# Where transposed and split operands begin inside their SBUF tiles

## The chip, the core and the metric

The kernel runs on one core of a Trainium2 chip. Its time is the device time of one execution in microseconds (us). The engines that matter are TensorE (matmuls, and loads of the stationary operand, which the profile lists apart as PE and PEld), VectorE (DVE), ScalarE (ACT), GpSimd (POOL) and the DMA queues. Operands lie in SBUF, a memory of 128 partitions; a place in it is a byte address that holds for all partitions alike.

## What is computed

One layer of an encoder on a sequence of 512 positions with 1024 features, in float32: a feed-forward, a mixer, a second feed-forward, each between two norms, with residuals.

```
def swiglu(x, w_in, w_out):
    gate, up = jnp.split(x @ w_in, 2, axis=-1)       # 1024 -> 2 x 2816
    return (jax.nn.silu(gate) * up) @ w_out          # 2816 -> 1024

h = swiglu(rmsnorm(x, norm_ffn1_pre), w_ffn1_in, w_ffn1_out)
x = x + 0.5 * rmsnorm(h, norm_ffn1_post)
h = mixer(rmsnorm(x, norm_mix_pre), w_mix_in, ...)   # gated convolution and 4 mLSTM heads
x = x + rmsnorm(h, norm_mix_post)
h = swiglu(rmsnorm(x, norm_ffn2_pre), w_ffn2_in, w_ffn2_out)
x = x + 0.5 * rmsnorm(h, norm_ffn2_post)
```

The mixer multiplies its input by w_mix_in (1024 x 3088), makes y of a gated convolution (512 features) and of the heads (512 features), and multiplies y (512 x 1024) by w_mix_out.

## The kernel before

**Arithmetic.** Every large product is made of float32r matmuls: an operand is split in a high part (a cast on ScalarE, line 366) and a low part (a subtraction on VectorE, line 369), and high x high, high x low and low x high are summed in PSUM. Most products are in addition cut by Strassen's scheme, seven half-size products in place of eight.

**The matmuls, by line.** A matmul has a moving operand, whose columns stream through, and a stationary operand of 128 x 128, which is loaded first.

- L545 (`plain`) and L519 (`mm_part`) in the feed-forward: the moving operand is 256 columns of the transposed x, the stationary one a weight tile. x is kept in tiles of four rows (`q`) for each half of the features and of the sequence; a row holds 256 columns of the high part and then 256 of the low part. The loop over k goes through the four rows in turn. `xq_tile` hands these tiles out.
- L519 in `seven` and L510 (`mm_cols`) in the mixer: the same for the mixer's transposed x, with 256 and 512 columns. High and low parts have a tile each, marked by "m" in the dictionary.
- L953 (the mixer's v and gates): here the mixer's x is stationary, and the moving operand is a weight tile of rows of 528 columns, taken as 256 and 272 columns.
- L726 (`product_out`), the feed-forward's second product: the stationary operand is a "left factor", a split sum of blocks of the hidden layer, made by `left_a` and `left_b` into tiles from `halves`; the moving operand is 512 columns of the output weights. Two sets of left factors (i = 2 in `left_a` and i = 0 in `left_b`) lie in the pool of the residual instead (named xl in the profile).
- L748 (`mm_out`): the rest of that product without Strassen's scheme, its hidden blocks split into tiles `hs`.
- L1428: the mixer's output, with y stationary (`yc` of the convolution, `ym` of the heads) and 512 columns of w_mix_out moving.

**Order.** Matmuls of the feed-forward stand in the program's order where they are pinned; elsewhere a scheduler orders each engine's instructions when the program is built. DMAs of weights are issued from SP's queue, some of them from GpSimd's, ahead of use into a pool of four tiles (`raw`), and the splits go to a pool of twelve (`whi`, `wlo`, `ws`).

**Where tiles lie.** All these tiles have fixed buffers. The pool `big` has 13 buffers of four rows of 528 float32 (BW = 528), since the mixer's v weights need rows of 528. `bigt` takes the first 2048 columns of such a buffer as four rows of 512; `wide` gives the whole of it. The feed-forward's x takes `wide` as four rows of 528. The built program places the pools as follows, the same in both versions:

| pool | first byte of the first buffer | bytes from one buffer to the next | first byte modulo 256, all buffers |
|---|---|---|---|
| big (x, left factors, rest, y, v weights) | 24256 | 8448 | 192 |
| weights (whi, wlo, ws, wt) | 134080 | 4096 | 192 |
| residual and xl | 7872 | 4096 | 192 |

Stationary tiles of a weight buffer lie 512 bytes apart, so all of them start at 192 modulo 256.

The functions that the diff touches, and their callers:

Of the kernel before, what the change touches and what calls it, by code (L numbers as in the profile page):

```python
# [8 lines left out]
F32 = mybir.dt.float32  # L9
F32R = mybir.dt.float32r  # L10
# [26 lines left out]
BW = 528  # L37
# [4 lines left out]
def encoder_kernel(ctx: ExitStack, tc: tile.TileContext, a: dict, out: bass.AP):  # L42
# [16 lines left out]
    def nm(s):  # L59
        uid[0] += 1  # L60
        return f"{s}_{uid[0]}"

    def wide(dt=F32):
        return big.tile([P, 4 * BW], dt, tag="big", name=nm("big"))

    def bigt(dt=F32):
        return wide(dt)[:, 0:2048].rearrange("p (q f) -> p q f", q=4)

    def ps():
        return psum.tile([P, 512], F32, tag="ps", name=nm("ps"))  # L70
# [229 lines left out]
    def w_get(ahead=2):  # L300
        w_split(max(0, 1 + ahead - len(ready)))
        return ready.pop(0)


    def xtile():
        return xpool.tile([P, D], F32, tag="x", name=nm("x"))
# [58 lines left out]
    def split(hi, lo, src, eng=nc.vector):  # L365
        latest["hi"] = nc.scalar.copy(out=hi, in_=src)  # L366
        if pinned["act"]:
            pin(latest["hi"])
        latest["lo"] = eng.tensor_tensor(out=lo, in0=src, in1=f32(hi), op=ALU.subtract)  # L369
        pin(latest["lo"])  # L370
# [33 lines left out]

    def xq_tile(xq, key):
        if key not in xq["q"]:
            xq["q"][key] = bigt(F32R) if "m" in xq else wide(F32R).rearrange("p (q f) -> p q f", q=4)
        return xq["q"][key]

    def xq_hl(xq, key):  # L410
# [112 lines left out]
    def ffn(xq, between, finish, mid=None, within=None, ahead=(2, 2, 1, 1), late=None, prep=None, block=0):  # L523
# [56 lines left out]
        def hcol(k):  # L580
            return h[k // 4][:, k % 4, 0:512]
# [3 lines left out]

        def halves(g):
            if g == 1:
                t = bigt(F32R).rearrange("p q f -> p (q f)")
                return t[:, 0:1024].rearrange("p (g f) -> p g f", g=1), t[:, 1024:2048].rearrange("p (g f) -> p g f", g=1)
            return tuple(  # L590
                bigt(F32R).rearrange("p q f -> p (q f)")[:, 0:2048].rearrange("p (g f) -> p g f", g=2) for _ in range(2))

        def each(v, g):
            return [v[:, i] for i in range(g)]
# [9 lines left out]
        def left_a(i, home=None):  # L604
            g, a_, b_ = group(i)
            if home is None:
                hi, lo = halves(g)

                def put(c, v):
                    split_free(hi[:, :, c:c + v.shape[2]], lo[:, :, c:c + v.shape[2]], v)  # L610

                hi_, lo_ = each(hi, g), each(lo, g)
            else:
                hi_, lo_ = home

                def put(c, v):
                    for e in range(g):
                        split_free(hi_[e][:, c:c + v.shape[2]], lo_[e][:, c:c + v.shape[2]], v[:, e])

            def step1():  # L620
                s1 = t4()[:, 0:256 * g].rearrange("p (g f) -> p g f", g=g)
                tt(s1, a_[:, :, early], b_[:, :, early], ALU.subtract)
                put(256, s1)

            def step2():
                put(0, a_[:, :, later])
                tt(a_[:, :, early], a_[:, :, later], a_[:, :, early], ALU.subtract)

            def step3():
                tt(a_[:, :, later], a_[:, :, early], b_[:, :, early], ALU.add)  # L630
                put(768, a_[:, :, later])

            def step4():
                put(512, a_[:, :, early])

            out_ = parts(hi_, lo_, g, {1: 0, 5: 256, 7: 512, 6: 768})
            if home is not None:
                return [step1, step2, step3, step4], out_
            s1 = t4()[:, 0:256 * g].rearrange("p (g f) -> p g f", g=g)
            tt(s1, a_[:, :, early], b_[:, :, early], ALU.subtract)  # L640
            put(0, a_[:, :, later])
            tt(a_[:, :, early], a_[:, :, later], a_[:, :, early], ALU.subtract)
            tt(a_[:, :, later], a_[:, :, early], b_[:, :, early], ALU.add)
            put(256, s1)
            put(512, a_)
            return out_
# [72 lines left out]
        def product_out(n, left, right, first, last_):  # L719
            tb, half = bank[n]  # L720
            for t in range(2):
                if n == 4:
                    first = (t, 0) not in begun
                    begun.add((t, 0))
                for x, y in ((0, 0), (0, 1), (1, 0)):
                    nc.tensor.matmul(  # L726
                        acc[tb + t][half], left[n][x][:, blk(t)], right[n][y], start=first and x == y == 0,
                        stop=last_ and x == 1, skip_group_check=True)

        def taken(n):  # L730

            for t in range(2):
                o = acc[bank[n][0] + t][bank[n][1]]
                e12, e22, e21 = extra[2 + t, 1], extra[t, 1], extra[t, 0]
                if n == 1:
                    nc.scalar.copy(e12, o)
                elif n == 5:
                    tt(e22, o, e21, ALU.subtract, lambda v: (pin(v), mark.update(taken=v)))
                elif n == 6:
                    tt(e12, o, e12, ALU.subtract, pin)  # L740
                else:
                    tt(e21, o, e12, ALU.subtract, pin)

        def mm_out(tb, half, k, hT, w):
            fresh = (tb, half) not in begun
            begun.add((tb, half))
            for hh, ww in ((0, 0), (0, 1), (1, 0)):
                nc.tensor.matmul(  # L748
                    acc[tb][half], hT[hh][:, blk(tb)], w[ww][:, blk(half, 512)],
                    start=fresh and hh == ww == 0, stop=k == NF - 1 and hh == 1, skip_group_check=True)  # L750
# [13 lines left out]
        hs, plain_n = None, 0  # L764
        marks = []
        ks = {}
        for at, (kind, n) in enumerate(order):
            if kind == "k":
                if plain_n % 2 == 0:
                    hs = bigt(F32R)  # L770
                q = 2 * (plain_n % 2)
                plain_n += 1
                hT = (hs[:, q, 0:512], hs[:, q + 1, 0:512])
                split(hT[0], hT[1], hcol(n))
                ks[n] = (hT, w_get(min(2, len(order) - 1 - at)))
                if plain_n == 1 and mid:
                    mid()
                if n < NF - tail:
                    for tb, half in ((2, 0), (3, 0), (0, 1), (1, 1), (0, 0), (1, 0), (2, 1), (3, 1)):
                        mm_out(tb, half, n, *ks[n])  # L780
            elif kind == "a":
                marks.append(latest["lo"].ins)
                if n % 2 == 0 and n:
                    if n in soon:
                        lefts = soon[n]
                    else:
                        with tc.issue_after(marks[n - LAG]):
                            lefts = left_a(n)
                left, right = lefts[n % 2], w_get(1)
                for m in ((1, 6, 7, 5) if n else (6, 7, 5)):  # L790
                    product_out(m, left, right, n == 0, n == seven - 1)
                    if n == seven - 1:
                        taken(m)
                if n == TURN:
                    homes = [xpool.tile([P, D], F32R, tag="x", name=nm("xl")) for _ in range(4)]
                    with tc.issue_after(marks[n]):
                        soon["b"] = left_b(0, (homes[0:2], homes[2:4]))
            else:
                if n == 0:
                    lefts = soon["b"]  # L800
                elif n % 2 == 0:
                    with tc.issue_after(mark["taken"].ins):
                        lefts = left_b(n)
                left, right = lefts[n % 2], w_get(2)
                for m in (2, 3, 4):
                    product_out(m, left, right, False, False)
                if n == 1:
                    for tb in range(NT):
                        x_t[tb] = xtile()
                        nc.gpsimd.dma_start(x_t[tb], x_src[block][tb])  # L810
# [110 lines left out]
    def within1(tb):  # L921
        if tb >= 2:
            flip_m(tb - 2, st[tb - 2], st["xq"])

    ffn(
        xT1,
        {
# [4 lines left out]
    xq = st["xq"]  # L932
# [2 lines left out]
        return xq_hl(xq, (k // 4, tb // 2))[hl][:, k % 4, blk(tb % 2)]  # L935


    vaug = wide().rearrange("p (q f) -> p q f", q=4)
    vv = vaug.rearrange("p c (h e) -> p c h e", e=BW // 4)
    nc.gpsimd.memset(vv[:, :, :, DV:DV + 1], 1.0)  # L940
    spread = t2()
# [308 lines left out]
        pn2[:, 256:272], parl, acd.rearrange("p q c -> p (q c)"),  # L1250
        start=True, stop=True,
    )
    Ct = wide().rearrange("p (q f) -> p q f", q=4)
    Cf = Ct.rearrange("p q f -> p (q f)")
    Cs = Cf[:, 0:12 * 129].rearrange("p (q i e) -> p q i e", q=4, i=3)
    nat1 = Cf[:, 1552:2064].rearrange("p (c r) -> p c r", r=P)
# [8 lines left out]
    weigh_k()  # L1265
    weigh_q()
    plain_o(3)
    ym = (bigt(F32R), bigt(F32R))
    yc = (bigt(F32R), bigt(F32R))

    hs = {}

# [199 lines left out]
```

## Time and profile before

| | |
|---|---|
| median of 3 runs | 885.02 us (884.16 to 885.32) |
| profiled execution | 884.01 us, span of its instructions 882.1 us |
| mean granted TensorE clock | 0.998 |
| instructions | 15403, of them 6039 matmuls and 6039 loads of a stationary operand |
| DMA | 123.24 MB, mean 140 GB/s |

The span goes through the first feed-forward (to about 341 us, its second product from 232 us), the mixer (to about 546 us) and the second feed-forward (second product from 765 us). In rows of groups the number behind x counts instructions, and then come the busy time in us and the mean duration of one in ns. Matmuls overlap in the pipeline, so the mean duration of one is longer than the step from one to the next. In the chain in order of time a row is: start in us, length in us, engine, tile and line, count.

### The profile page before, as it was taken

To read this page: it belongs to the slowest core of one execution; us is meant where nothing else is said; L and a number is where in the kernel's file an instruction comes from. 1 tells how busy PE (TensorE), PEld (TensorE's weight loads), DVE (VectorE), ACT (ScalarE), POOL (GpSimd) and SP (SyncE) were. 2 spreads that over 40 slices of the span, in tenths; PEclk is the share of its full clock that TensorE was granted. 3 is DMA by queue.
4 is the path that set the end of the run, shared out by engine and by line. 5 is a ranking of instruction groups with operands and counts; after the bars stand their busy time and mean duration, and the time that the engine had idled before them with its cause. 6 is when DMAs were issued, how large, how long until landed. Compare 5 with 4: busy or idle time off the path is not lost.

```text
span 882.1 us, 15403 instructions
## 1 busy us (share of the span) xinstructions
PE 873.4 (99%) x6039; PEld 808.1 (92%) x6039; DVE 731.5 (83%) x1159; ACT 492.9 (56%) x855; POOL 93.6 (11%) x123
## 2 busy tenths in 40 slices
PE   8999999999999999999999999999999999999997
PEld 7999999999988889988998988999999999988885
DVE  7989898988889978887588757897898888869956
ACT  7655556544657645755475536555555555546722
POOL 5000000001232023100121011000000000223000
PEclk9999999999999999999999999999999999999999
DMA  9444333435998852442063733433333423899722
GB/s 263 121 121 134 106 95 98 120 88 130 227 246 200 279 180 86 121 119 72 1 191 96 223 112 106 130 100 97 96 96 98 138 77 109 202 243 229 268 74 95
DMA packets 140384, 123.24 MB, mean 140 GB/s; under 512 B 5500, under 2 KB 116112, under 8 KB 140312
## 3 DMA queue, kind: packets, MB, share of 16 engines
q1 hardware_dynamic: 129936, 97.62, 37.0%
q0 software_dynamic: 10368, 24.65, 12.6%
q8 instruction: 47, 0.77, 0.4%
q14 instruction: 25, 0.20, 0.1%
q10 hardware_dynamic: 8, 0.01, 0.0%
HBM read 115.96 MB, written 6.29 MB: 139 GB/s over the span
## 4 chain that ended last, share of the span: by engine, by line
PE 98%; DVE 0%; ACT 0%; issue 0%; POOL 0%; DVEq 0%; POOLq 0%; ACTq 0%
PE ps L519 48%; PE ps L726 19%; PE ps L510 9%; PE ps L545 5%; PE ps L1428 5%; PE ps L748 5%; PE ps L953 3%; PE ps L1331 1%; PE ps L422 1%; PE ps L1339 0%; PE ps L475 0%; PE ps L1280 0%; PE ps L1307 0%; PE ps L1300 0%; PE ps L1373 0%
## 5 line engine op out<-in xcount | busy, mean ns | idle before, releaser
L519 PE MATMUL ps<-big,whi 128*128 128x256 f32 x2064 | 284.1, 281 | 0.0
L519 PEld LDWEIGHTS ps<-big,whi 128*128 128x128 f32 x2064 | 261.4, 188 | 1.1 <-ACT t L1312 0.2
L366 ACT CAST whi<-raw 128x1024 fp32r<-128x1024 f32 x170 | 175.6, 1051 | 68.5 <-DVE raw L219 23.7
L369 DVE TENSOR_TENSOR wlo<-raw,whi 128x1024 fp32r<-128x1024 f32 x166 | 201.1, 1218 | 12.1 <-ACT whi L366 7.8
L519 PE MATMUL ps<-big,wlo 128*128 128x256 f32 x1032 | 161.8, 280 | 0.0
L519 PEld LDWEIGHTS ps<-big,wlo 128*128 128x128 f32 x1032 | 139.0, 189 | 0.0
L726 PE MATMUL ps<-whi,big 128*128 128x512 f32 x336 | 105.7, 389 | 0.0
L726 PEld LDWEIGHTS ps<-whi,big 128*128 128x128 f32 x336 | 62.9, 188 | 13.0
L519 PE MATMUL ps<-big,ws 128*128 128x256 f32 x516 | 70.0, 280 | 0.0
L173 POOL DMA_DIRECT2D raw<-in_w_ffn_out_dram x18 | 22.2, 1232 | 442.3 <-DMA raw<-in_w_ffn_out_dram 226.3
L519 PEld LDWEIGHTS ps<-big,ws 128*128 128x128 f32 x516 | 64.8, 188 | 0.0
L726 PE MATMUL ps<-wlo,big 128*128 128x512 f32 x168 | 64.8, 389 | 0.0
L693 ACT COPY t<-ps 128x256 f32<-128x256 f32 x40 | 14.9, 373 | 88.4 <-PE ps L519 88.4
L510 PE MATMUL ps<-big,whi 128*128 128x512 f32 x224 | 54.5, 394 | 0.0
L366 ACT CAST whi<-t 128x1024 fp32r<-128x1024 f32 (+1 forms) x44 | 39.5, 914 | 17.7 <-DVE t L219 10.2
L510 PEld LDWEIGHTS ps<-big,whi 128*128 128x128 f32 x224 | 41.4, 188 | 8.7
L369 DVE TENSOR_TENSOR wlo<-t,whi 128x1024 fp32r<-128x1024 f32 (+1 forms) x44 | 46.1, 1048 | 1.4 <-ACT whi L366 0.7
L748 PE MATMUL ps<-whi,big 128*128 128x512 f32 x128 | 39.8, 390 | 0.0
L726 PEld LDWEIGHTS ps<-wlo,big 128*128 128x128 f32 x168 | 31.5, 188 | 6.5
L695 DVE TENSOR_TENSOR t<-ps,t 128x256 f32<-128x256 f32 x40 | 16.9, 422 | 21.0 <-PE ps L519 20.9
L545 PE MATMUL ps<-big,whi 128*128 128x256 f32 x256 | 33.6, 282 | 0.0
L698 ACT ACTIVATE t<-t 128x512 f32<-128x512 f32 x40 | 25.2, 631 | 12.4 <-DVE t L695 12.0
(245 smaller groups left out, 1412.3 us busy)
## 6 DMA issues: line engine op xcount, KB each, us to landing
raw<-in_w_ffn_in_dram SPq DMA_DIRECT2D x68, 512.0 KB, 4.8
raw<-in_w_ffn_out_dram SPq DMA_DIRECT2D x26, 512.0 KB, 4.2
raw<-in_w_mix_in_dram SPq DMA_DIRECT2D x24, 512.0 KB, 4.2
t<-in_w_ffn_in_dram SPq DMA_DIRECT2D x20, 512.0 KB, 3.8
raw<-in_w_ffn_out_dram SPq DMA_DIRECT2D x36, 256.0 KB, 5.0
raw<-in_w_ffn_out_dram POOLq DMA_DIRECT2D x18, 512.0 KB, 7.8
xd<-x POOLq DMA_DIRECT2D x8, 512.0 KB, 2.9
x<-xd POOLq DMA_DIRECT2D x8, 512.0 KB, 5.2
```

The lines of the kernel that those rows point to most:

```text
L173: nc.gpsimd.dma_start(sums.rearrange("p (g f) -> p g f", g=2), top[:, 512:1024].rearrange("p (g f) -> p g f", g=1).broadcast_to([P, 2, 512 ...
L366: latest["hi"] = nc.scalar.copy(out=hi, in_=src)
L369: latest["lo"] = eng.tensor_tensor(out=lo, in0=src, in1=f32(hi), op=ALU.subtract)
L510: nc.tensor.matmul(o, w[ww][:, k, :], xq_tile(xq, (k // 4, xx))[:, k % 4, FULL], start=n == 0, stop=n == 3 * KD - 1)
L519: pin(nc.tensor.matmul(o, ww[:, k, :], x[xx][:, k, :], start=first and n == 0, stop=n == 11, skip_group_check=True))
L545: pin(nc.tensor.matmul(o, ww[:, k, :], xq_hl(xq, (k // 4, th))[xx][:, k % 4, :], start=n == 0, stop=n == 3 * KD - 1))
L695: nc.vector.tensor_tensor(out=c[:, h1], in0=y[:, h0], in1=a_[:, h1], op=ALU.add)
L698: mark["act"] = nc.scalar.activation(c, c, AF.Silu)
L726: nc.tensor.matmul(acc[tb + t][half], left[n][x][:, blk(t)], right[n][y], start=first and x == y == 0, stop=last_ and x == 1, skip_group_c ...
L748: nc.tensor.matmul(acc[tb][half], hT[hh][:, blk(tb)], w[ww][:, blk(half, 512)], start=fresh and hh == ww == 0, stop=k == NF - 1 and hh == ...
L953: nc.tensor.matmul(pv_[i][:, 0:at.stop - at.start], xv(xx, k, tb), ww[:, k % 2, at], start=n == 0, stop=n == 3 * KD - 1)
L1428: nc.tensor.matmul(acc[half], yy[yi][:, k % 4, blk(tb)], wmo[k][wi][:, blk(half, 512)], start=(n == 0 and yi == 0 and wi == 0), stop=(n == ...
```

## The change

`bigt` gets a start `at` (in float32 columns; 1 column is 4 bytes) and a length `row` of a row. Five kinds of tiles begin later in their buffer: the feed-forward's x by 48 columns (192 bytes), the mixer's x and the left factors of `halves` by 8 (32 bytes), the plain rest by 24 (96 bytes), the mixer's y by 40 (160 bytes). The feed-forward's x gets rows of 512 columns, where it had rows of 528. The two places that took `wide` as four rows of 528 (`vaug`, `Ct`) say the same through `bigt(row=BW)`. On every engine the instructions stand in the same order as before, with the same waits.

```diff
@@ wide, bigt
-    def bigt(dt=F32):
-        return wide(dt)[:, 0:2048].rearrange("p (q f) -> p q f", q=4)
+    def bigt(dt=F32, at=0, row=512):
+        return wide(dt)[:, at:at + 4 * row].rearrange("p (q f) -> p q f", q=4)
@@ xq_tile
-            xq["q"][key] = bigt(F32R) if "m" in xq else wide(F32R).rearrange("p (q f) -> p q f", q=4)
+            xq["q"][key] = bigt(F32R, at=8) if "m" in xq else bigt(F32R, at=48)
@@ ffn, halves
-                t = bigt(F32R).rearrange("p q f -> p (q f)")
+                t = bigt(F32R, at=8).rearrange("p q f -> p (q f)")
...
-                bigt(F32R).rearrange("p q f -> p (q f)")[:, 0:2048].rearrange("p (g f) -> p g f", g=2) for _ in range(2))
+                bigt(F32R, at=8).rearrange("p q f -> p (q f)")[:, 0:2048].rearrange("p (g f) -> p g f", g=2) for _ in range(2))
@@ ffn, plain rest
-                    hs = bigt(F32R)
+                    hs = bigt(F32R, at=24)
@@ mixer
-    vaug = wide().rearrange("p (q f) -> p q f", q=4)
+    vaug = bigt(row=BW)
...
-    Ct = wide().rearrange("p (q f) -> p q f", q=4)
+    Ct = bigt(row=BW)
...
-    ym = (bigt(F32R), bigt(F32R))
-    yc = (bigt(F32R), bigt(F32R))
+    ym = (bigt(F32R, at=40), bigt(F32R, at=40))
+    yc = (bigt(F32R, at=40), bigt(F32R, at=40))
```

Start addresses modulo 256 of the operands concerned, from the built programs:

| matmuls | moving operand | stationary operand | moving minus stationary, before | after |
|---|---|---|---|---|
| L519, L545, feed-forward | x | weights, 192 | 0, 64, 128, 192 in turn | 192 |
| L519, L510, mixer | mixer's x | weights, 192 | 0 | 32 |
| L953 | v weights | mixer's x | 0, 64, 128, 192 in the mix 4, 4, 2, 2 of twelve | 224, 32, 96, 160 in the same mix |
| L726, left factor from `halves` | weights, 192 | left factor | 0 | 224 |
| L726, left factor in xl | weights, 192 | xl | 0 | 0 |
| L748 | weights, 192 | plain rest | 0 | 160 |
| L1428 | weights or big, 192 | y | 0 | 96 |

## The prediction

> **What bounds the kernel now.** I read the page's busy shares first, then the waits of TensorE, then the chain of work that ended last.
>
> ```profile
> PE 873.4 (99%) x6039; PEld 808.1 (92%) x6039; DVE 731.5 (83%) x1159; ACT 492.9 (56%) x855; POOL 93.6 (11%) x123
> PE 98%; DVE 0%; ACT 0%; issue 0%; POOL 0%; DVEq 0%; POOLq 0%; ACTq 0%
> PE ps L356 <- POOL gbias L880: 1.4, 1, 1.4
> PE ps L422 <- DVE t L467: 1.1, 2, 0.6
> ```
>
> TensorE is busy 99% of the span, the chain is TensorE to 98%, and its only listed waits come to 2.5 us. So the time is the number of matmuls times the step from one matmul's start to the next one's. The change neither adds, removes nor reorders an instruction on any engine; it moves bytes within tiles. It can move the time only through that step. A busy TensorE is not one at its peak: the durations of single matmuls overlap, so I don't use them. The step comes from the pieces of the chain, which give a start, a length and a count:
>
> ```profile
> 35.93 196.41 PE ps L519 x1668
> 547.21 10.34 PE ps L545 x88
> 484.99 8.64 PE ps L519 x72
> 343.07 8.76 PE ps L953 x72
> 374.94 26.78 PE ps L510 x118
> 236.51 83.00 PE ps L726 x366
> 854.13 21.77 PE ps L748 x96
> 500.96 21.79 PE ps L1428 x96
> ```
>
> Length by count: a 256-column matmul on the feed-forward's x takes 117.75 ns in L519 and 117.5 ns in L545. The same line, the same shape, on the mixer's x (at 484.99) takes 120.0 ns. The 512-column matmuls take 226.9, 226.8, 226.8 and 227.0 ns. One column is thus (227.0 - 120.0) / 256 = 0.418 ns, and 256 columns are 107.0 ns; what stands above that is about 13 ns for 256 columns and for 512 alike, and 10.5 ns on the feed-forward's x. That excess, paid once for each matmul, is what this change works on.
>
> What happens once for each matmul is the load of the next stationary operand:
>
> ```profile
> 300.30 0.39 PE L726 MATMUL ps<-wlo,big 128*128 128x512 f32 x1
> 300.31 0.19 PEld L726 LDWEIGHTS ps<-whi,big 128*128 128x128 f32 x1
> 300.53 0.39 PE L726 MATMUL ps<-whi,big 128*128 128x512 f32 x1
> 300.53 0.19 PEld L726 LDWEIGHTS ps<-wlo,big 128*128 128x128 f32 x1
> ```
>
> The load of the next one begins with the matmul, so two streams read SBUF side by side: the moving operand's columns and the next stationary tile. The place table of the section on the kernel gives their start addresses. I call "distance" the moving operand's start minus the start of the stationary tile then being loaded, modulo 256. On the mixer's x, and in all 512-column matmuls, the distance is 0. On the feed-forward's x it runs 0, 64, 128, 192 from one matmul to the next, because a row of that tile is 2112 bytes. That is the one difference that I find between the 120.0 and the 117.5 ns: an address effect of 2.5 ns on the step is in this trace already.
>
> Excess goes lower elsewhere. Six bf16 matmuls of 256 columns, and the plain f32 matmuls of 129 columns:
>
> ```profile
> 8.29 0.82 PE L356 MATMUL ps<-rawg 128*128 128x256 bf16 x6
> 436.97 1.78 PE ps L1331 x16
> 476.26 1.78 PE ps L1331 x16
> ```
>
> Taking a last duration of 0.28 us off 0.82 leaves 0.54 for five steps, 108 to 109 ns. The f32 ones take 111 ns a record, for head 0 (436.97), whose moving operand starts at a multiple of 64 bytes, and for head 3 (476.26), where it starts 48 bytes past one: there an offset below 64 bytes changes nothing. They are two records to a matmul, so their stream is slower for each column, and I use them as a neighbour only.
>
> **The change part by part.** Five groups of matmuls get other distances; the counts are those of the groups by line and form:
>
> ```profile
> L519 PE MATMUL ps<-big,whi 128*128 128x256 f32 x2064 | 284.1, 281 | 0.0
> L510 PE MATMUL ps<-big,whi 128*128 128x512 f32 x224 | 54.5, 394 | 0.0
> L545 PE MATMUL ps<-big,whi 128*128 128x256 f32 x256 | 33.6, 282 | 0.0
> L726 PE MATMUL ps<-whi,big 128*128 128x512 f32 x336 | 105.7, 389 | 0.0
> L748 PE MATMUL ps<-whi,big 128*128 128x512 f32 x128 | 39.8, 390 | 0.0
> L1428 PE MATMUL ps<-whi,big 128*128 128x512 f32 x80 | 26.0, 390 | 0.0
> ```
>
> These are the groups with the high parts; with the low parts and sums the lines hold 3612, 336, 384, 756, 192 and 192 (of L726's, 168 have a stationary operand in another pool, which stays). Of L519's, 252 are the mixer's (three pairs of column blocks, 84 each), 3360 the feed-forward's. With L545 the feed-forward's x has 3744 matmuls, 3744 x 117.7 = 441 us: half the span.
>
> *The feed-forward's x* (48 words, and rows of 512 words in place of 528). Its distance becomes 192 at every matmul. What does a matmul at distance 192 cost? Two groups mix distances in known shares. A full run of twelve on the feed-forward's x, three at each distance:
>
> ```profile
> 203.93 1.57 PE L519 MATMUL ps<-big,ws 128*128 128x256 f32 x12
> 205.34 1.10 PE L519 MATMUL ps<-big,whi 128*128 128x256 f32 x8
> ```
>
> From 203.93 to 205.34 are 1.41 us, 117.5 ns each, so the four distances sum to 470.0. The mixer's L953 takes 8.76 / 72 = 121.7 ns; half of its matmuls have 272 columns, 16 x 0.418 = 6.7 ns more, so 118.3 ns at 256 columns. Of twelve, its distances are four times 0, four times 64, two times 128 and two times 192. With 120.0 for distance 0: the other three sum to 350.0, and 480 + 4a + 2(350.0 - a) = 1420 gives a = 120 for distance 64, and 230 for 128 and 192 together, 115 each. If cost goes by distance alone, x falls from 117.5 to 115: 3744 x 2.5 = 9.4 us less. The split of the 230 is open: with one at the floor of 109, the other is 121. So the term is bounded by 3744 x 8.5 = 31.8 us less and 3744 x 3.5 = 13.1 us more; I take the even split, since nothing in the rows prefers either.
>
> *Left factors, plain rest, mixer's y and mixer's x.* These go from distance 0 to distances 224 (588 of L726), 160 (192 of L748), 96 (192 of L1428) and 32 (336 of L510 and 252 of L519), 1560 matmuls. No full-rate matmul of this trace has a distance that isn't a multiple of 64. Nearest rows: the mean of the three distances other than 0 is 350.0 / 3 = 116.7, 3.3 ns under distance 0, so 1560 x 3.3 = 5.2 us less; and L1331, where a shift below 64 bytes brought nothing. I take half, 2.6 us. Bounds: 1560 x 11 = 17.2 us less (down to 109 ns), and, since a distance of 32 could be as much above 120 as the others are below, 5.2 us more.
>
> *L953* (192) now meets distances 224, 32, 96, 160 instead of 0, 64, 128, 192. At a mean of 117.5 in place of 118.3 this is 0.2 us: nothing.
>
> *Writers of the moved tiles.* ScalarE's casts and VectorE's subtractions write the same count of elements. Cost nothing, hidden under TensorE: in the stages of the two big loops VectorE has slack.
>
> ```profile
> 36.00:232.00 196.00, 196.00 (x1667) 196.00 (x1666) 172.50 (x273) 103.43 (x169) 5.01 (x4) 1.00 0.42 117
> 237.00:319.00 82.00, 82.00 (x363) 67.86 (x363) 72.65 (x99) 50.76 (x72) 19.73 (x25) 1.00 0.91 245
> ```
>
> VectorE, the third busy time of a row, is at 172.5 of 196 us (88%) and 72.65 of 82 (89%); TensorE would have to gain 11% before VectorE set the pace, and the forecast is 2.1% and 1.5%. In the second stretch the DMA engines are 91% busy, the tightest cover; all that TensorE gains there is 366 x 1.7 = 0.6 us.
>
> Sum: 9.4 + 2.6 = 12.0 us, off the profiled execution's 884.0 (span 882.1 and 1.9 around it): 872.0. The median of the runs is 885.0, 1.0 above it, so **873 us**.
>
> A rule speaks against this. The Trainium skill, "TensorE: Matmul & The Clock Gate", section "Step-by-step: what each phase is for", says that TensorE has two independent SBUF read ports, so that loading the next tile's weights takes no read bandwidth from the running matmul; by it the step could not depend on a distance, the sum would be 0, and the time 885. The 120.0 against 117.5 ns at one line and shape does not agree with it. The same page, section "Back-to-back issue gap", gives N/2.4 + 2.5 ns for a warm matmul, by an estimate 109 ns at 256 columns; the bf16 row agrees, no float32r row here does.
>
> **The rivals.**
>
> *Slower: a constant distance is the price, not its value.* The 120.0 ns stands where the distance is the same at every matmul; the 117.5 where it walks by 64. If it is the walk that avoids trouble, rows of 512 words take it away, and x pays 120.0: 3744 x 2.5 = 9.4 us more, less the 2.6 above: 885.0 + 6.8 = 892. Where the other terms bring nothing, 894. For it: every constant distance in the trace is at the top price. Against: all of those have the value 0, and L953, which repeats each distance twice, is nearer to 117.5 than to 120. It decides when x costs more than 117.5 + 2.6 / 3744 us, 118.2 ns.
>
> *Nothing moves:* the 2.5 ns has another cause that the mixer's stage has in itself, or a stream's order decides and not addresses: 885. Against it: all 512-column groups, before, in and after the mixer, carry the 13 ns as well. The skill's rule of two ports, above, would give this case.
>
> *More than forecast:* a shift by half of 64 bytes takes the two streams apart altogether, and the 1560 matmuls fall to the floor, 17.2 us, with x's 9.4: 885.0 - 26.6 = 858. For it: the bf16 step. Against: L1331's 111 ns at every offset.
>
> *The gain is taken back by a late engine:* VectorE's 88% says no; I count it with the second rival.
>
> **How the numbers follow.** The forecast 0.60, its own range 863 to 881 (x between 113 and 117, the others between 0 and 5.2 us); the slower rival 0.18, spread 886 to 895; nothing 0.10; more than forecast 0.12, spread 850 to 863. A difference under 0.2%, 1.8 us, can't be told from none: between 883.2 and 886.8 is "same". Faster 0.72, same 0.10, slower 0.18. The range 857 to 890 leaves out the lower half of the fast rival and the greater part of the slow one, and so under 2 in 10.
>
> **What would show it.** Length by count for L519 in the feed-forward: 115 is the forecast, 120 the slower rival, 117.7 no effect. L545 must follow it. L726's 168 matmuls with the other pool's stationary operand must stay at 226.8, and those with moved ones fall to about 225; L748, L1428 and L510 likewise. Counts and engines' busy times, but for TensorE's, must stay. The prediction is wrong if x's step rises, or if gaps on TensorE with VectorE as releaser appear in the feed-forward's loop.

## The result

The changed kernel takes 878.0 us (median of 20 executions, 876.1 to 885.6) against 885.1 before. The ratio of the means, 880.3 to 885.2 us, is 0.9944 (95% interval 0.9922 to 0.9967). That is 4.9 us less by the means and 7.1 by the medians, where 12 were forecast (873). The median hides something: the kernel has two times. Twelve executions lie at 876.1 to 878.7 us, eight at 884.4 to 885.6, none between, and the granted TensorE clock is 0.998 or 0.999 in all of them. The kernel before has one time, 884.2 to 886.7 us, but for one execution of 1076.3 us that is left out of its mean and stays unexplained. The profiled execution of the changed kernel is one of the long ones (885.3, span 883.4), and that turns out to be useful, since it shows both behaviours in one trace.

The chain of TensorE's work, in order of time, in the changed kernel's profile (start in us, length in us, line, count of matmuls), to be held against the same rows of before:

```profile
36.58 196.46 PE ps L519 x1668
237.25 84.91 PE ps L726 x366
346.40 8.83 PE ps L953 x72
378.57 27.54 PE ps L510 x118
490.63 8.40 PE ps L519 x72
506.47 22.40 PE ps L1428 x96
567.05 10.88 PE ps L545 x96
577.93 186.33 PE ps L519 x1644
773.99 80.70 PE ps L726 x348
854.69 22.51 PE ps L748 x96
```

Of the kernel before, the second feed-forward's rows are these:

```profile
560.79 11.28 PE ps L545 x96
572.07 193.44 PE ps L519 x1644
```

Length by count gives the step from one matmul to the next:

| group | distance before, after | step before, ns | step after, ns |
|---|---|---|---|
| L519, first feed-forward | 0 to 192 in turn, 192 | 117.75 | 117.8 |
| L519, second feed-forward (193.44 us for 1644 before) | the same | 117.7 | **113.3** |
| L545, second feed-forward (last 96; 11.28 us before) | the same | 117.5 | 113.3 |
| L519, mixer | 0, 32 | 120.0 | 116.7 |
| L726, all left factors | 0, 224 (168 of 756: 0) | 226.8 | 232.0 |
| L510 | 0, 32 | 226.9 | 233.4 |
| L1428 | 0, 96 | 227.0 | 233.3 |
| L748 | 0, 160 | 226.8 | 234.5 |
| L953 | 0 to 192, 32 to 224, mixed | 121.7 | 122.6 |

Two things show. The same line with the same distances takes 113.3 ns in one feed-forward and 117.8 in the other. And every 512-column group with a new distance has become slower, by 6 to 8 ns for a matmul. The 168 matmuls of L726 whose stationary operand lies in xl, which didn't move, are the built-in control. In the groups by line and form (mean duration of one behind the comma) they stand at 390 ns, where they had 389; the moved ones rose from 389 to 395. The first line is of the kernel before, the others are of the changed one:

```profile
L726 PE MATMUL ps<-whi,xl 128*128 128x512 f32 x96 | 30.9, 389 | 0.0
L726 PE MATMUL ps<-whi,big 128*128 128x512 f32 x336 | 107.7, 395 | 0.0
L726 PE MATMUL ps<-whi,xl 128*128 128x512 f32 x96 | 31.0, 390 | 0.0
L748 PE MATMUL ps<-whi,big 128*128 128x512 f32 x128 | 40.8, 397 | 0.0
```

Counts are equal, and VectorE's busy time is 731.5 us as before. In this execution TensorE has one wait in the mixer that the kernel before did not have, for VectorE at the end of a chain that goes back to a transfer of weights:

```profile
PE ps L519 <- DVE t L1089: 0.6, 1, 0.6
```

The balance, from the steps: L726 756 x 5.2 = 3.9 us more, L510 336 x 6.5 = 2.2, L1428 192 x 6.3 = 1.2, L748 192 x 7.7 = 1.5, together 8.8 us lost; the mixer's L519 252 x 3.3 = 0.8 us won. The second feed-forward's x won 1872 x 4.4 = 8.2 us, the first nothing in this execution. That makes 0.2 us less, where the span of the profiled execution is 1.3 us longer than that of before (883.4 to 882.1). The rest is the wait of 0.6 us, the later start of the first loop (36.58 to 35.93, 0.65 us) and L953's 192 x 0.9 = 0.2 us. If the first feed-forward also takes 113.3 ns, another 8 us go, and the time is 877: the short one. So the long time, which looks like no effect, is a gain and a loss that cancel.

### The profile page after: what moved, and what is told of

Its sections match the earlier page's. It is cut to its first block, busy times and chain, and to the rows that moved or that the text cites. A ratio compares the mean times of both kernels' runs of the same rounds, so it can differ in the third digit from the quotient of the medians.

```text
span 883.4 us, 15403 instructions
## 1 busy us (share of the span) xinstructions
PE 873.5 (99%) x6039; PEld 799.6 (91%) x6039; DVE 731.5 (83%) x1159; ACT 492.3 (56%) x855; POOL 91.0 (10%) x123
## 4 chain that ended last, share of the span: by engine, by line
PE 96%; DMA 1%; DVE 1%; issue 0%; ACT 0%; POOL 0%; DVEq 0%; POOLq 0%; ACTq 0%
PE ps L519 46%; PE ps L726 20%; PE ps L510 9%; PE ps L748 5%; PE ps L545 5%; PE ps L1428 5%; PE ps L953 3%; DMA raw<-in_w_mix_in_dram 1%; PE ps L422 1%; PE ps L1331 1%; DMA g_row<-in_norm_ffn_pre_dram 0%; PE ps L475 0%; PE ps L1339 0%; PE ps L1280 0%; PE ps L1373 0%
## 5 line engine op out<-in xcount | busy, mean ns | idle before, releaser
L519 PE MATMUL ps<-big,whi 128*128 128x256 f32 x2064 | 279.8, 279 | 0.6 <-DVE t L1089 0.6
L519 PEld LDWEIGHTS ps<-big,whi 128*128 128x128 f32 x2064 | 257.4, 188 | 2.2 <-DVE t L1089 1.1
L519 PE MATMUL ps<-big,wlo 128*128 128x256 f32 x1032 | 159.7, 279 | 0.0
L519 PEld LDWEIGHTS ps<-big,wlo 128*128 128x128 f32 x1032 | 137.5, 189 | 0.0
L726 PE MATMUL ps<-whi,big 128*128 128x512 f32 x336 | 107.7, 395 | 0.0
L726 PEld LDWEIGHTS ps<-whi,big 128*128 128x128 f32 x336 | 63.0, 188 | 14.9
L519 PE MATMUL ps<-big,ws 128*128 128x256 f32 x516 | 68.9, 279 | 0.0
L726 PE MATMUL ps<-wlo,big 128*128 128x512 f32 x168 | 65.8, 396 | 0.0
L519 PEld LDWEIGHTS ps<-big,ws 128*128 128x128 f32 x516 | 63.9, 188 | 0.0
L510 PE MATMUL ps<-big,whi 128*128 128x512 f32 x224 | 55.5, 398 | 0.0
L510 PEld LDWEIGHTS ps<-big,whi 128*128 128x128 f32 x224 | 41.3, 188 | 9.7
L748 PE MATMUL ps<-whi,big 128*128 128x512 f32 x128 | 40.8, 397 | 0.0
L726 PEld LDWEIGHTS ps<-wlo,big 128*128 128x128 f32 x168 | 31.6, 188 | 7.5
L545 PE MATMUL ps<-big,whi 128*128 128x256 f32 x256 | 33.1, 280 | 0.0
```

The costliest lines, as they stand in the source:

```text
L510: nc.tensor.matmul(o, w[ww][:, k, :], xq_tile(xq, (k // 4, xx))[:, k % 4, FULL], start=n == 0, stop=n == 3 * KD - 1)
L519: pin(nc.tensor.matmul(o, ww[:, k, :], x[xx][:, k, :], start=first and n == 0, stop=n == 11, skip_group_check=True))
L545: pin(nc.tensor.matmul(o, ww[:, k, :], xq_hl(xq, (k // 4, th))[xx][:, k % 4, :], start=n == 0, stop=n == 3 * KD - 1))
L726: nc.tensor.matmul(acc[tb + t][half], left[n][x][:, blk(t)], right[n][y], start=first and x == y == 0, stop=last_ and x == 1, skip_group_c ...
L748: nc.tensor.matmul(acc[tb][half], hT[hh][:, blk(tb)], w[ww][:, blk(half, 512)], start=fresh and hh == ww == 0, stop=k == NF - 1 and hh == ...
```

## The experiments

Theory when they began: two streams read SBUF side by side, the moving operand and the next stationary tile, and the step goes by their distance, for each group by itself; a stage in which x has distance 192 settles on one of two steps. Rivals: the groups act on each other; the place or the row length of x counts, not a distance; the two times come from elsewhere.

All kernels are the changed kernel with its numbers made constants, one pair for the two feed-forwards where there are two, and with the same order of instructions on every engine, but for the three that change it, as told there:

```diff
+X_AT, X_ROW, M_AT = (48, 48), (512, 512), 8
+L_AT, R_AT, Y_AT = (8, 8), (24, 24), 40
...
-            xq["q"][key] = bigt(F32R, at=8) if "m" in xq else bigt(F32R, at=48)
+            xq["q"][key] = bigt(F32R, at=M_AT) if "m" in xq else bigt(F32R, at=X_AT[xq["b"]], row=X_ROW[xq["b"]])
```

and so on for `halves` (L_AT), the plain rest (R_AT) and y (Y_AT). The distance of x and of the mixer's x is 4 x at, that of the others 256 - 4 x at.

### x alone, and the rest alone

```diff
-X_AT, X_ROW, M_AT = (48, 48), (512, 512), 8
-L_AT, R_AT, Y_AT = (8, 8), (24, 24), 40
+X_AT, X_ROW, M_AT = (48, 48), (512, 512), 0
+L_AT, R_AT, Y_AT = (0, 0), (0, 0), 0
```

> The feed-forward's x as in the changed kernel (48 columns, rows of 512); the mixer's x, left factors, plain rest and y back at the start of their buffers. Theory (the step goes by the distance between the moving operand and the tile being loaded, group by group): L519 and L545 as in the changed kernel, 113.3 ns in a stage that has settled there and 117.8 in one that has not; all 512-column groups back at 227 ns, which the changed kernel had at 233 to 234 (8.8 us), the mixer's 252 of L519 back at 120 (0.8 us more). So 8 us under the changed kernel: 869 us where both feed-forwards settle low, 877 where one does not. Rival (the groups act on each other, the shifts of one make the other's gain possible): not under 876.

Measured: 873.45 us, a ratio of 0.9867 (0.9834 to 0.9899), again in two groups: 868.9, 869.7, 870.1 and 876.8, 877.3, 877.8. In the profile, of an execution of 868.9, both feed-forwards and the 512-column groups stand where the theory had them:

```profile
35.99 189.04 PE ps L519 x1668
229.18 82.96 PE ps L726 x366
367.56 26.78 PE ps L510 x118
564.27 186.32 PE ps L519 x1644
839.11 21.77 PE ps L748 x96
```

113.3 ns in both, 226.7 to 227 ns in the others. The rival said not under 876, so it falls.

The counterpart has x as before and all the other shifts (`X_AT, X_ROW, M_AT = (0, 0), (528, 528), 8`, the second line as in the changed kernel).

> The feed-forward's x as before (rows of 528, at the start of the buffer); the mixer's x, left factors, plain rest and y shifted as in the changed kernel. Theory: x at 117.5 to 117.8 ns as before, the 512-column groups at 233 to 234, the mixer's L519 at 116.7: 885 + 8.8 - 0.8 = 893 us, and one time, not two. Rival (the shifts below 64 bytes are harmless by themselves, what was lost came with the new x): 885.

Measured: 893.66 us, 1.0095 (1.0082 to 1.0108), one time (892.7 to 894.4). The shifts of the other groups cost 8.3 us by themselves, whether x is moved or not.

### Is it the distance?

Rows of 512 without a shift (`X_AT = (0, 0)`, all else 0):

> Rows of 512 for the feed-forward's x, no shift anywhere: the distance is 0 at every matmul. Theory: L519 and L545 at 120.0 ns, as on the mixer's x before: 885 + 3744 x 2.3 ns = 894 us. Rival (rows of 512 by themselves bring the gain, whatever the start): 113 to 118 ns, 868 to 885 us.

Measured: 893.86 us, 1.0100 (1.0085 to 1.0114), and 120.0 ns in both feed-forwards:

```profile
37.09 200.16 PE ps L519 x1668
577.70 197.28 PE ps L519 x1644
```

So rows of 512 bring nothing; 192 bytes more in the start turn 120.0 into 113.3. This is still the place of x as well as its distance. The next kernel reaches the same distances the other way round, by moving the weights:

```diff
-    wpool = ctx.enter_context(tc.tile_pool(name="wpool", bufs=12))
+    gap = ctx.enter_context(tc.tile_pool(name="gap", bufs=1)); gap.tile([P, 16], F32, name="gap"); wpool = ctx.enter_context(tc.tile_pool(name="wpool", bufs=12))
...
+X_AT, X_ROW, M_AT = (0, 0), (512, 512), 16
+L_AT, R_AT, Y_AT = (16, 16), (16, 16), 16
```

> The other way to the same distances: the pool of weights moves up by 64 bytes as a whole, the feed-forward's x stays at the start of its buffer with rows of 512 (distance 192), and left factors of the pool big, plain rest, y and the mixer's x move up by 64 bytes with the weights (distance 0). Theory (only the difference of the two starts counts): as with x alone shifted, 113.3 or 117.8 ns on the feed-forward's x, 226.7 ns on these 512-column groups; the 168 of L726 with a stationary operand in xl now have distance 64 and take 229. So 869 or 877 us. Rival (the place of x in its buffer counts by itself): 120.0 ns on x, as in the kernel with rows of 512 and no shift, 894 us.

Measured: 869.7 us in both executions. x begins at the very addresses at which it took 120.0 ns, and takes 113.3:

```profile
36.07 189.04 PE ps L519 x1668
312.45 16.78 PE ps L748 x74
564.66 186.32 PE ps L519 x1644
839.77 21.77 PE ps L748 x96
```

What counts is the difference of the two starts, not either of them. The differences in the two kernels, 192 bytes more for x and 64 bytes more for the weights, are 256 apart, so counting them modulo 256 is borne out by this pair. The 168 matmuls of L726 with xl, which went from distance 0 to 64, take 229.0 ns, as expected. (A part of the mixer's output, whose moving operand is in the pool that did not move, got distance 192 here and rose to 233 ns.)

### The map of distances

Three kernels with another distance for each group, and two with x alone, were run once each, for the steps in their profiles (892.3, 892.4, 896.1, 878.0 and 888.0 us):

```diff
+X_AT, X_ROW, M_AT = (16, 32), (512, 512), 48     # e4: L_AT, R_AT, Y_AT = (16, 48), (32, 16), 48
+X_AT, X_ROW, M_AT = (44, 52), (512, 512), 4      # e6: L_AT, R_AT, Y_AT = (4, 60), (2, 62), 6
+X_AT, X_ROW, M_AT = (56, 40), (512, 512), 60     # e7: L_AT, R_AT, Y_AT = (12, 52), (20, 44), 28
+X_AT, X_ROW, M_AT = (12, 28), (512, 512), 0      # e11: all others 0
+X_AT, X_ROW, M_AT = (20, 36), (512, 512), 0      # e12: all others 0
```

> Shifts by multiples of 64 bytes alone, another one for each group, to read one step for each distance from the profile. Rows of 512 for x; first feed-forward's x at distance 64, second's at 128; left factors at distances 192 (first) and 64 (second); plain rest 128 (first), 192 (second); y 64; mixer's x moving 192. Theory: by the sums used in the prediction with 113.3 ns put in for 192, x at 64 takes 120 and at 128 takes 116.7; the 512-column groups at 64, 128, 192 go under 227 ns, since it is the part of the distance below 64 that made them 233. Rival (a 512-column matmul pays for any distance that is not 0): 233 ns in them too.

> More distances, read as steps from the profile. Feed-forward's x at distance 176 (first) and 208 (second); left factors at 240 (first) and 16 (second); plain rest 248 (first), 8 (second); y 232; mixer's x 16. Theory (two streams that meet in the same piece of memory, so the step changes gradually with the distance): x between 113 and 118 on both sides of 192; 512 columns between 226.7 and 233 near 0, on both sides. Rival (distances that are multiples of 64 are special): x off 192 jumps to 120, 512 columns to 233 or more as soon as the distance is not 0.

> More distances. Feed-forward's x at distance 224 (first) and 160 (second); left factors at 208 (first) and 48 (second); plain rest 176 (first), 80 (second); y 144; mixer's x 240. Theory: x at 224 and 160 has 116 to 119 ns, 512 columns 229 to 235 everywhere, none under 226.7. Rival (512 columns have a low place too, as 256 columns have at 192, only elsewhere): one of these under 226.

> x alone shifted, rows of 512, to the distances between the ones tried: 48 in the first feed-forward, 112 in the second. Theory (192 is one of few distances at which the two streams can run clear of each other; the others seen lie at 116.7 to 120): 116 to 120 ns in both, 879 to 894 us. Rival (a second low distance exists that a stage can't miss): 113 or 114 ns in one of them.

> The same with distance 80 in the first feed-forward and 144 in the second. Theory: 116 to 120 ns in both, 879 to 894 us. Rival: 113 or 114 ns in one of them.

The rows of the first, third and fourth that carry the readings below:

```profile
322.72 17.19 PE ps L748 x74
489.63 8.17 PE ps L519 x72
505.20 21.97 PE ps L1428 x96
861.60 22.42 PE ps L748 x96
```

```profile
36.67 197.38 PE ps L519 x1668
580.74 195.09 PE ps L519 x1644
865.92 22.10 PE ps L748 x96
```

```profile
36.74 197.38 PE ps L519 x1668
573.09 186.32 PE ps L519 x1644
```

L748 at distance 128 takes 232.3 ns, at 192 233.5 and at 80 230.2; L1428 at 64 takes 228.9; the mixer's L519 at 192 takes 113.5; x at 224 and at 48 takes 118.3, at 160 118.7. In the last, the second feed-forward has distance 112 and takes 113.3 ns. All steps read in this way, in ns, for matmuls with the same distance throughout:

| distance | 256 columns | 512 columns |
|---|---|---|
| 0 | 120.0 | 226.7 |
| 8 | | 233.3 (L748) |
| 16 | 113.5 to 120.0 (mixer, by piece) | 226.7 (L726), 231.7 (L510) |
| 32 | 116.7 (mixer) | 233.3 |
| 48 | 118.3 | 231.8 |
| 64 | 117.8 | 229.0 |
| 80 | 118.3 | 230.1 |
| 96 | | 233.3 |
| 112 | 113.3 | |
| 128 | 118.7 | 232.3 |
| 144 | 118.6 | 233.2 |
| 160 | 118.7 | 234.3 |
| 176 | 119.3 | 232.0 |
| 192 | 113.3 or 117.8 | 233.2 |
| 208 | 119.2 | 233.3 |
| 224 | 118.3 | 233.3 |
| 232 | | 230.2 |
| 240 | 117.2 (mixer) | 227.5 (L726), 235.7 (L510) |
| 248 | | 230.7 |

My expectation for the first of these kernels, that multiples of 64 would lower the 512-column groups, fell: its rival held, and they pay at nearly every distance that isn't 0. Its x took 117.8 and 118.7 ns, where I had 120 and 116.7. No distance took them under 226.7, as expected of the third, and against its rival. For 256 columns it is the other way: 0 is the dearest place of all, 192 and 112 are low, and 16 is low in some pieces of the mixer. The gradual course around a place, expected of the second kernel, holds near 0 for L726 and nowhere else: x jumps from 113.3 at 192 to above 119 at 176 and 208. The fourth contradicted its theory and showed the second low distance; the fifth held to it. At 16 and at 240 L726 and L510 differ by 5 and 8 ns at the same distance and width, so the distance alone doesn't fix the step of a group.

The two steps of one distance can be seen at work in the changed kernel's first feed-forward (matmuls of L545 in order of time: start, length, count):

```profile
23.97 1.07 PE L545 MATMUL ps<-big,wlo 128*128 128x256 f32 x8
24.88 2.28 PE L545 MATMUL ps<-big,whi 128*128 128x256 f32 x16
26.99 1.11 PE L545 MATMUL ps<-big,wlo 128*128 128x256 f32 x8
27.93 0.28 PE L545 MATMUL ps<-big,whi 128*128 128x256 f32 x1
```

From 23.97 to 24.88, eight matmuls in 0.91 us, 114 ns. Then there is a short stop at about 26 us, in which TensorE waits for a low part from VectorE. From 26.99 to 27.93, 0.94 us, 117.5 ns, and so for all of the 1750 that follow without a break.

### What draws the step

That stop was the suspect. This kernel has x alone shifted, and takes the stop away by asking for the low parts later; the scheduler's order changes with it in the first feed-forward:

```diff
-            for ww, xx in ((hi, 0), (hi, 1), (lo, 0)):
+            for ww, xx in ((hi, 0), (lo, 0), (hi, 1)) if th else ((hi, 0), (hi, 1), (lo, 0)):
```

> The kernel with x alone shifted, and one order changed: in the second half of the plain columns (L545) the products of the weights' low part come ahead of those of x's low part, so that TensorE asks for the low parts of x's last block 8 matmuls (0.9 us) later. That is where TensorE waits for VectorE at about 26 us, the last stop before the 1750 matmuls of the first feed-forward's loop. Theory (a stage keeps the step that it falls into at its last stop, and without that stop the first feed-forward goes on from the transposes into 113.3 ns, as the second one always has): one time, 869 us, in all runs. Rival (the step is drawn by something else, such as when the transfers land): two times, 869 and 877, as before.

Measured: five executions at 868.3 to 870.3 us, but one at 877.9. The theory of one last stop falls. Two more kernels were run: the same order in the kernel before, and the same order with x and part of the mixer's x shifted. The edit of the second, beside the order:

```diff
-bigt(F32R, at=M_AT) if "m" in xq
+bigt(F32R, at=M_AT if isinstance(key, tuple) else T_AT) if "m" in xq      # T_AT = 48
```

> The kernel before with that order alone changed, nothing shifted. Theory: the stop at 26 us goes, 0.1 to 0.3 us, and the step stays 117.5 to 117.8: 885 us. Rival (the order itself is worth the 8 us): 877.

Measured: 884.9 us, 1.000 (0.9991 to 1.0009): the order is worth nothing by itself.

> The same and, in the mixer, the four tiles t1 to t4 that L519 alone reads shifted by 192 bytes (144 of its 252 matmuls); the ones that L510 reads too stay at distance 0. Theory: these 144 at 113.3 to 117.8 instead of 120, 0.3 to 1.0 us, so 868 us. Rival (steps of mixed distances, twelve at a time, follow no rule of that kind): no difference.

Measured: three executions at 868.4 to 869.5 and three at 875.9 to 877.2 us; a gain from the mixer can't be told within that. The profile is of a long one:

```profile
21.91 1.04 PE L422 MATMUL ps<-ident,t 128*128 128x128 f32 x8
22.70 1.19 PE L545 MATMUL ps<-big,whi 128*128 128x256 f32 x8
23.73 1.11 PE L545 MATMUL ps<-big,wlo 128*128 128x256 f32 x8
24.67 1.10 PE L545 MATMUL ps<-big,whi 128*128 128x256 f32 x8
25.61 1.10 PE L545 MATMUL ps<-big,wlo 128*128 128x256 f32 x8
26.55 0.63 PE L545 MATMUL ps<-big,whi 128*128 128x256 f32 x4
```

There is no stop at 26 us any more. The 117.5 ns (0.94 us for eight) stand from the transposes of L422 on. So, as far as these traces show, a step is drawn anew at a stop or at a run of transposes, and kept in an unbroken row of matmuls. The second kernel of the map agrees: at distance 16 its mixer has an unbroken row of 46 matmuls at 120 ns from 427 us on, and this one at 113.5:

```profile
489.95 8.17 PE ps L519 x72
```

(They read different tiles, and one profile can't tell a draw from a difference between tiles.) What draws the step is not settled. Of the 40 executions with x at distance 192, in all five kernels that have it, 15 have the long time; in both of these that were profiled it is the first feed-forward that has the high step, and the second has the low one in all five profiles.

### Distance 112

If 112 is like 192, it has two times also. `X_AT = (28, 28)`, all others 0:

> x alone shifted, to distance 112 in both feed-forwards, the distance at which the second one took 113.4 ns. Theory (112 is like 192: two steps, and the first feed-forward, which stops and starts several times, falls into either): two times, about 869 us and one 4 to 10 us longer. Rival (at 112 there is one step alone, so that the first feed-forward can't miss it): 869 us in all runs, and the two times of the changed kernel come from its distance, not from the stage.

Measured: 868.9 to 870.2 us in all five executions, median 869.46, 0.9821 (0.9808 to 0.9835). One time: the rival held. The steps from one start to the next, worked out from the matmuls' records in this kernel's trace, show why. The first 22 matmuls behind the transposes at 22 us, in ns:

```
201, 117, 119, 114, 120, 120, 115, 118, 121, 119, 113, 114, 113, 113, 114, 113, 113, 114, 113, 113, 114, 113
```

After some ten matmuls they come to 113 and stay there. The stop follows, here of 0.5 us, and behind it the same happens again. At 192 a row can also begin with up to five matmuls of 114 to 123 ns ahead of the 113, but where the step was 117.5 it was so almost from the start of the row, and no row was seen to leave it.

The last kernel adds 112 in the mixer (the edit above with `T_AT = 28`):

> x at distance 112 in both feed-forwards, and in the mixer the four tiles t1 to t4 that L519 alone reads at 112 too; the rest unshifted. Theory (112 leads to one step): one time again, in all runs; the mixer's 144 matmuls at 113.3 to 116.7 in place of 120, 0.5 to 1.0 us, so 868.5 to 869. Rival (the five runs at 112 were luck: 15 of the 40 executions with x at distance 192 so far were 8 us longer): about two of the six runs at 877.

Measured: 868.6 to 869.6 us, median 869.22, 0.9823 (0.9810 to 0.9837). Ten executions of ten at distance 112 have the short time. If each were a draw at the rate of 192, 15 long ones of 40, the chance of that would be 0.625 to the power of 10, under 1%. The 0.5 to 1.0 us expected of the mixer did not come: 72 of its matmuls take 8.51 us where they took 8.64, over all 252 the mean step falls from 119.7 to 118.4 ns, 0.3 us, and the two kernels can't be told apart by their times. This version and the one before it beat the changed kernel by 9 us and the kernel before by 16.

## Why the prediction was half right

**What bounds the kernel: right.** TensorE's step times the count is the time. The gains and losses of the steps appeared in the time nearly in full (with x alone at distance 112, 15.8 us of the 16.5 that its steps give); what another engine took back was 0.6 us, in one stop of the changed kernel's profile.

**Distance as the cause: right, and shown.** Moving the weights gave what moving x gave, and x at one and the same start lost 6.7 ns of its step when the distance changed. The Trainium skill, "TensorE: Matmul & The Clock Gate", section "Step-by-step: what each phase is for", says that loading the next weights takes no read bandwidth from the running matmul. Read as in the prediction, that the step can't depend on a distance, this doesn't agree with these float32r matmuls (120.0 ns at distance 0, 113.3 at 192 and 112). Whether the loads take bandwidth is not shown by that: no run left them out.

**x's term: right in kind, mis-sized.** The step that put 115 ns on distance 192 was the even split of "230 for 128 and 192 together". The sum was nearly right, measured 118.7 + 113.3 = 232.0; the split is uneven. For distance 64 the equations gave 120 where 117.8 was measured. That miss comes in with L953: the four steps measured one by one (120.0, 117.8, 118.7, 113.3) add up to 469.8, as the walk did to 470.0, but give L953 a mean of 117.9 ns at 256 columns, where its row had given 118.3. Times twelve and halved, these 0.4 ns are the 2.2. Whether a mix of distances costs the sum of its parts was not tested. With 113.3 ns the term is 3744 x 4.4 = 16.5 us, not 9.4. But it has two values, and half of it, the first feed-forward's, came in 12 of 20 executions only (by their times). Nothing in the trace of before told of that.

**The other groups' term: wrong in sign.** The failed step is the one that carried a gain from 256 columns to 512: the mean 116.7 of the distances other than 0, "3.3 ns under distance 0", half of it taken. Both widths had the same 13 ns above their columns, and I took it for the same excess, to be lowered in the same way. The runs show that 0 is the dearest distance for 256 columns and the cheapest for 512. The 1308 matmuls of 512 columns that moved lost 8.8 us; my bound on that side, 5.2 us for all 1560, was a mirror of the gain and not read from any row, and it was too near. The mixer's 252 of 256 columns did gain 3.3 ns each, as the mean said. I had no row of 512 columns at any distance but 0, and that should have widened the bound on the loss. That the median, 878.0, still lies near the forecast is luck: x's gain was too small in the forecast and the others' loss was missing, and the two errors offset each other.

**The rivals.** "A constant distance is the price": refuted by 113.3 ns at a constant 192; what it would have seen as proof, 120.0 with rows of 512, needs distance 0. "Nothing moves": refuted, though eight executions have its time. "More than forecast", with the 512-column groups at the floor: the opposite happened. A rival in which x gains and the others lose was missing, though the two terms were separate.

**The sum.** Forecast 9.4 + 2.6 = 12.0 us less. Measured 8.2 or 16.5 less for x, 8.8 more for 512 columns and 0.8 less in the mixer: 0.2 or 8.5 us less, which are the two times.

## What to carry to other kernels

Where TensorE is busy throughout, time the step from one matmul's start to the next for each shape, and compare groups whose operands start at different addresses: a difference of a few ns at one shape can be worth per cents (here 4.4 ns on half the span, 1.8%). Shift one group at a time and read its step in the profile, since what helps 256 columns can cost 512 columns: distance 192 brings the first 6.7 ns against distance 0 and costs the second 6.5. Run a candidate often enough to see whether its times fall into groups; a median can stand between two behaviours, and the better choice may be the start that has one of them only.

## What the hardware showed that was not expected

- Float32r matmuls have a step that depends on where the moving operand starts relative to the stationary tiles: 113.3 to 120.0 ns for 256 columns, 226.7 to 235.7 for 512. The address of either alone doesn't decide. A matmul's own stationary tile and the next one, which loads meanwhile, start alike modulo 256 in nearly all of these matmuls, so the runs don't tell which of the two counts.
- At one distance there can be two steps, 113.3 and 117.8 ns at 192, kept for 1750 matmuls (8 us). From one to the other they were seen to change at stops and transposes only. At 112 there was one, reached within about ten matmuls. What chooses between the two remains open.
- The dearest distance for 256 columns, 0, is the cheapest for 512 of those tried. Why is open too: no run took the loads away from under the matmuls.
